# Branch A of a two-branch encoder layer: softmax sums divided out behind the value products, and GpSimd taking over weight subtractions

## The chip, the cores and the metric

One core of one Trainium2 chip runs the whole layer. The metric is the device time of one launch in microseconds (us). A change of less than about 4 us (0.2%) is what a measurement of this kernel can hardly tell from none.

## What is computed

Two inputs, `x_prompt` (1024 tokens of width 1024) and `x_sample` (512 tokens), go through the same encoder layer in float32. Branch A, which the change concerns, is grouped-query attention with 8 query heads of width 64 and 2 key/value heads:

```python
xn = rmsnorm(x); z = xn @ w_in          # q_A | k_A | v_A | q_B | k_B | v_B | gate_A | gate_B
# branch A, per key/value head (2) and query head in its group (4):
s = einsum('bqkgd,bskd->bkgqs', q, k) * scale
p = softmax(s, axis=-1)
o_A = einsum('bkgqs,bskd->bqkgd', p, v)
# branch B: 8-head attention over a clamped 8 x 16 window, with a position bias
mix = (sigmoid(gate_A) * (o_A @ w_proj_a) + sigmoid(gate_B) * (o_B @ w_proj_b)) @ w_out
x = x + mix
x = x + relu(rmsnorm(x) @ w_up) ** 2 @ w_down        # followed by a last rmsnorm
```

## The kernel before

All large products run on TensorE (PE) with operands that are split in two: a high part rounded to the product's number format, and a low part, the rest. `split` makes them: ScalarE (ACT) copies the source into the high part, VectorE (DVE) subtracts that from the source. A product of two split operands is three matmuls (`mm3`, line 214), one with a split operand on one side is two.

`run` handles one input. The 512-token input goes first (its names end in `s0`, "short"), then the 1024-token input (`s1`, "long", where `NB` is 2). After both, an MLP stage of about half the run follows. For branch A, `run` goes twice through two phases, once for each key/value group g:

- phR (projection): per 128 tokens, `zs` = q and k and v of this group (24 matmuls), `zvs` = branch B's values (24 matmuls), the norm and rotation of q and k (`chain`: `us` on GpSimd (POOL), `ts` on DVE, `rrs` on ACT), and their transposition `pqs` on PE. `load_a(g)` loads and splits this group's q, k and v weights (`wghs` high, `wgls` low).
- phA (attention). A unit is one head and 512 queries (4 units of 4 tiles of 128 queries per group in s0, 8 in s1). `s_tile` makes scores `ss` of 128 queries in PSUM (lines 801, 802), DVE takes the row maximum (`nms`, 804), ACT the exponential into `ps` with the row sum `ls` (811), DVE the reciprocal `rls` (813), and GpSimd multiplies the 128 x T tile by it (814). For units with `qb` 0 (all of s0, half of s1), `t_chunk` transposes `ps` on PE (`pTs`, 838) 128 keys at a time; ACT copies the high part `pths` (841), DVE subtracts the low part `ptls` (842). For the other half of s1, `turn_a` transposes `ps` in 32 x 32 blocks on DVE (856), writes it to DRAM (`tas`) and `fetch_a` reads it back rearranged (`hqs`); `cut_a` splits it on ACT (887) and GpSimd (889). `pv` multiplies these by the values (`os`, 825 and 826), and `finish_o` adds the upper and lower half of `os` (copy on ACT 484, addition on DVE 494 into `ot_As`) and `put` writes the result to DRAM (`oads`), as a DMA that stands in ACT's queue (439).

Between these steps PE works on filler, the matmuls of gate A (`gpss`), which `gate` hands out in pieces of three; its weights (`w_gs`) are loaded and split chunk by chunk, the next one held back until the present one is under way. 

The code's order is not the order on the engines. A scheduling layer places each instruction on its engine by its own estimate of when inputs are there, then adds semaphores; instructions pinned by `keep_in_program_order` or `issue_after` hold their place. Each engine then runs its row strictly in order, SyncE (SP) and ACT their DMA issues too. A small change in phA thus moves instructions of all engines there and in the phase behind it. Tiles come from pools with a set number of buffers (`bufs`); an instruction that writes a buffer waits until its last reader is done.

Of the kernel before, what the change touches and what calls it, by code (L numbers as in the profile page):

```python
# [11 lines left out]
F32 = mybir.dt.float32  # L12
# [3 lines left out]
ALU = mybir.AluOpType  # L16
AX = mybir.AxisListType

P = 128
D = 1024  # L20
NC8 = D // P
HD = 64
# [39 lines left out]
def encoder(ctx: ExitStack, tc: tile.TileContext, xs, outs, w):  # L62
    nc = tc.nc
    dram = ctx.enter_context(tc.tile_pool(name="dram", bufs=1, space=bass.MemoryType.DRAM))
    cst = ctx.enter_context(tc.tile_pool(name="cst", bufs=1))
    sml = ctx.enter_context(tc.tile_pool(name="sml", bufs=8))
# [26 lines left out]
    def mm(name):  # L93
        return pmm.tile([P, 512], F32, tag="mm", name=name)
# [98 lines left out]
    def behind(engine):  # L193
# [3 lines left out]
            yield  # L197
        firm[engine].clear()

    def split(hi, lo, src, pin=False):  # L200
        op = nc.scalar.activation(hi, src, AF.Copy)
        note("ACT", op)
        if pin:
            tc.keep_in_program_order(op)
        n = src.shape[1]
        cut = [0, n // 2, n] if n % 2 == 0 else [0, n]
        for a, b in zip(cut, cut[1:]):
            op = nc.vector.tensor_tensor(lo[:, a:b], src[:, a:b], hi[:, a:b].bitcast(F32), op=ALU.subtract)  # L208
            if pin:
                tc.keep_in_program_order(op)  # L210
            note("DVE", op)
# [211 lines left out]
    def run(tr, nxt, first):  # L423
        N, x, T, NT, NB = tr.N, tr.x, tr.T, tr.NT, tr.NB
        xh, xl = tr.xh, tr.xl
        rows = T // GRID_W
# [4 lines left out]
        oad = dram.tile([4 * P, T], F32, name=f"oad{N}")  # L431
# [5 lines left out]
        def put(dst, src):  # L437
            if slot_no[0] is None:
                nc.scalar.dma_start(dst, src)
            else:  # L440
                later_put.append((slot_no[0], dst, src))
# [27 lines left out]
                    put(dst[c * P : (c + 1) * P, tb * 512 : tb * 512 + 512], sg)  # L469
                    yield  # L470

        def finish_o(o, n, dst, pool, nm, parts=None):

            both = len(o.shape) == 3
            cols = 2 * n if both else n
            t = pool.tile([P, cols], F32, tag="ot", name=f"ot_{nm}", bufs=2 if cols == 512 and both else 3)
            c, b = t[0:HD, 0:n], t[0:HD, cols - n : cols]
            if both:
                tv = t[0:HD].rearrange("p (i q) -> p i q", i=2)
                nc.scalar.activation(tv, o[HD:P], AF.Copy)  # L480
                nc.vector.tensor_tensor(tv, o[0:HD], tv, op=ALU.add)
                o = b
            else:
                nc.scalar.activation(c, o[HD:P, :n], AF.Copy)
                o = o[0:HD, :n]
            if parts is not None:
                hi, lo, ps = parts
                b = t[ps, cols - n : cols]
                nc.vector.tensor_tensor(b, o, c, op=ALU.add)
                nc.scalar.activation(hi, b, AF.Copy)  # L490
                op = nc.vector.tensor_tensor(lo, b, hi.bitcast(F32), op=ALU.subtract)
                last_sum[:] = [op.ins]
                return
            nc.vector.tensor_tensor(b, o, c, op=ALU.add)
            put(dst, b)


# [41 lines left out]
        for g in range(2):  # L539
            with phase(f"phR{N}_{g}") as ph:  # L540
# [29 lines left out]
                if first and fresh:  # L570
                    warm_up(4)
                    last_sub = []

                    def first_tile(parts):
                        def hi_of(kb):
                            hi, lo, src = parts[kb]
                            tc.keep_in_program_order(nc.scalar.activation(hi, src, AF.Copy))

                        def lo_of(kb, a):
                            hi, lo, src = (t[:, 2 * a : 2 * a + 2] for t in parts[kb])  # L580
                            tc.keep_in_program_order(
                                nc.vector.tensor_tensor(lo, src, hi.bitcast(F32), op=ALU.subtract)
                            )

                        hi_of(0)
                        tr.p0_t(0, xn_of[0], [partial(lo_of, 0, 0), partial(lo_of, 0, 1)])
                        hi_of(1)
                        lo_of(1, 0)
                        last_sub.append(partial(lo_of, 1, 1))
                        warm_up(4)  # L590

                    def more_x():
                        x23 = slot([P, 2, D], F32, f"x23{N}", True)
                        for i in range(2):
                            tc.keep_in_program_order(
                                nc.sync.dma_start(x23[:, i, :], x[(2 + i) * P : (3 + i) * P, :])
                            )
                            xt_of[2 + i] = x23[:, i, :]


                    def more_and_norm():
                        more_x()
                        xn_of[1] = tr.p0(1, ph, gb, x1.pop(), last_sub.pop())

                    wh, wl = load_a(g, lambda: x1.append(norm_load(x, 1, ph, f"{N}_1")), first_tile, more_and_norm)
                    tr.p0_t(1, xn_of.pop(1))
                    xn_of[2] = tr.p0(2, ph, gb, xt_of[2])
                else:
                    with tc.issue_after(ends) if g else ExitStack():
                        wh, wl = early.pop("a") if early else load_a(g)  # L610
                if g == 0 and first:
                    setup_tables()
                if early:
# [102 lines left out]
                for tt in range(NT):  # L716
                    tb, j = divmod(tt, 4)
                    nm = f"{N}_{g}_{tt}"
# [17 lines left out]
                    op = nc.sync.dma_start(rt, w["rope"][tt * P : (tt + 1) * P])  # L736
# [51 lines left out]
                setup_bias()  # L788
            with phase(f"phA{N}_{g}") as ph:
                units = [(h, qb) for h in range(4) for qb in range(NB)]  # L790
                PP = {}

                def s_tile(u, j):
                    h, qb = u
                    nm = f"{N}_{g}_{h}_{qb}_{j}"
                    q0 = (qb * 4 + j) * P
                    lhs = qT[h % 2][:, h // 2, q0 : q0 + P]
                    s = big(f"s{nm}")[:, :T]
                    for kb in range(NB):
                        ks = slice(kb * 512, kb * 512 + 512)  # L800
                        nc.tensor.matmul(s[:, ks], lhs, kT[:, 0, ks], start=True, stop=False)
                        nc.tensor.matmul(s[:, ks], lhs, kT[:, 1, ks], start=False, stop=True)  # L802
                    nm_ = sml.tile([P, 1], F32, tag="nm", name=f"nm{nm}")
                    nc.vector.tensor_reduce(nm_, s, axis=AX.X, op=ALU.max, negate=True)  # L804
                    p = ph.tile([P, T], F32, tag="P", name=f"p{nm}", bufs=8)
                    l = sml.tile([P, 1], F32, tag="l", name=f"l{nm}")
                    to, of = p, s
                    if NB == 2 and qb == 1:
                        to = p.rearrange("p (b k i) -> p k b i", b=4, i=32)
                        of = s.rearrange("p (k i b) -> p k b i", b=4, i=32)  # L810
                    op = nc.scalar.activation(to, of, AF.Exp, bias=nm_, accum_out=l)  # L811
                    rl = sml.tile([P, 1], F32, tag="rl", name=f"rl{nm}")
                    nc.vector.reciprocal(rl, l)  # L813
                    nc.gpsimd.tensor_scalar(p, p, rl, 1.0, op0=ALU.mult, op1=ALU.mult)  # L814
                    PP[u, j] = p
                    return op.ins

                o_of = {}

                def pv(u, kc, hi, lo):  # L820
                    h, qb = u
                    if kc == 0:
                        o_of[u] = mm(f"o{N}_{g}_{h}_{qb}")
                    o = o_of[u]
                    nc.tensor.matmul(o, vhl[:, kc, :], hi, start=(kc == 0), stop=False)
                    nc.tensor.matmul(o, vhl[:, kc, :], lo, start=False, stop=(kc == NT - 1))
                    if kc == NT - 1:
                        r0 = (g * 4 + h) * HD
                        finish_o(o, 512, oad[r0 : r0 + HD, qb * 512 : qb * 512 + 512], ph, f"A{N}_{g}_{h}_{qb}")

                queue = []
                LAG = 2
# [56 lines left out]
                        nc.gpsimd.tensor_tensor(lo[:, a], lo[:, a].bitcast(F32), hi[:, a].bitcast(F32), op=ALU.subtract)  # L889

                if NB == 2:
                    for u in ((0, 1), (0, 0)):
                        for j in range(4):
                            last_exp[:] = [step_s(u, j)]
                            fill.pull(1)
                    for i in range(3):
                        fetch_a((0, 1), i)
                    for h in range(4):
                        u, nn, nd = (h, 1), (h + 1, 0), (h + 1, 1)
# [14 lines left out]
                        for kc in range(NT):  # L914
# [6 lines left out]
                            hi, lo = (t[:, :, kc % 2 * 32 : kc % 2 * 32 + 32] for t in quarter[u, kc // 2])  # L921
# [5 lines left out]
                else:  # L927
# [4 lines left out]
                    for ui, u in enumerate(units):  # L932
                        h, qb = u
# [17 lines left out]
                fill.drain()  # L951
                for item in queue:
                    pv(*item)

        mA = {}
        wp_b = []
# [1140 lines left out]
```

## Time and profile before

| | |
|---|---|
| median of 3 runs | 2106.4 us (2104.5 to 2107.51) |
| the profiled execution | 2105.4 us, its span 2103.6 us |
| granted TensorE clock | 0.999 |
| busy share of the span | PE 99%, DVE 70%, ACT 54%, POOL 21% |
| phA of s0, g 0 and 1 | about 50 to 98 us and 124 to 166 us of the span |
| phA of s1, g 0 and 1 | about 447 to 560 us and 635 to 760 us |
| phR between them | about 98 to 124 us and 560 to 635 us |

PE is nearly always occupied, so time can come only from the moments in which it waits. The profile lists who waited for whom: "PEld" is PE's weight load, which stands in the same row as the matmuls and goes ahead of its matmul. Matmuls overlap and their ends are modelled, so a wait that the weight load shows can be hidden, in the column of PE itself, under the recorded length of the matmul before. 1.8 us of the 2105.4 lie outside the span.

### The profile page before, as it was taken

To read this page: it belongs to the slowest core of one execution; us is meant where nothing else is said; L and a number is where in the kernel's file an instruction comes from. 1 tells how busy PE (TensorE), PEld (TensorE's weight loads), DVE (VectorE), ACT (ScalarE), POOL (GpSimd) and SP (SyncE) were. 2 spreads that over 40 slices of the span, in tenths; PEclk is the share of its full clock that TensorE was granted. 3 is DMA by queue.
4 is the path that set the end of the run, shared out by engine and by line. 5 is a ranking of instruction groups with operands and counts; after the bars stand their busy time and mean duration, and the time that the engine had idled before them with its cause. 6 is when DMAs were issued, how large, how long until landed. Compare 5 with 4: busy or idle time off the path is not lost. (4 is left out here: it accounts for less than half of the span.)

```text
span 2103.6 us, 31314 instructions
## 1 busy us (share of the span) xinstructions
PE 2072.8 (99%) x10615; PEld 1809.0 (86%) x10615; DVE 1477.5 (70%) x2761; ACT 1142.2 (54%) x2455; POOL 445.6 (21%) x510
## 2 busy tenths in 40 slices
PE   9999999999999999999999999999999999999998
PEld 8887878987797778888888999999999988888886
DVE  6665786778648747778854877787777777669563
ACT  6664753667566745566423556565556634334442
POOL 2232310338435823543102100011000000000000
PEclk9999999999999999999999999999999999999999
DMA  6437557557626866877553666478445899788561
GB/s 193 136 101 209 158 165 253 182 135 191 171 65 182 208 170 198 235 225 219 181 182 131 196 195 206 153 240 223 145 155 161 283 342 348 214 273 277 159 209 61
DMA packets 406758, 406.45 MB, mean 193 GB/s; under 512 B 97599, under 2 KB 333767, under 8 KB 406599
## 3 DMA queue, kind: packets, MB, share of 16 engines
q1 hardware_dynamic: 368119, 339.16, 52.8%
q10 hardware_dynamic: 31328, 45.11, 6.4%
q0 software_dynamic: 7152, 20.19, 3.5%
q8 instruction: 84, 1.38, 0.3%
q14 instruction: 75, 0.61, 0.1%
HBM read 291.06 MB, written 114.10 MB: 193 GB/s over the span
## 5 line engine op out<-in xcount | busy, mean ns | idle before, releaser
L214 PE MATMUL dn<-wd,ah 128*128 128x512 f32 x1248 | 384.4, 389 | 0.0
L214 PEld LDWEIGHTS dn<-wd,ah 128*128 128x128 f32 x1248 | 234.2, 188 | 48.7
L214 PE MATMUL dn<-wd,al 128*128 128x512 f32 x624 | 242.8, 389 | 0.0
L1571 ACT ACTIVATE ah<-ar 128x512 fp32r<-128x512 f32 x168 | 104.1, 627 | 203.3 <-PE dn L214 184.3
L214 PE MATMUL gpss<-xs_0h,w_gs 128*128 128x512 f32 x512 | 186.1, 400 | 0.3 <-DVE w_gs L208 0.2
L1572 DVE TENSOR_TENSOR al<-ar,ah 128x512 fp32r<-128x512 f32 x168 | 113.9, 686 | 71.6 <-ACT ah L1571 64.7
L214 PE MATMUL ud<-B,A 128*128 128x384 f32 x768 | 143.6, 334 | 0.7 <-DVE c L1689 0.7
L214 PE MATMUL uc<-B,A 128*128 128x384 f32 x768 | 143.7, 334 | 0.0
L214 PE MATMUL ua<-B,A 128*128 128x384 f32 x768 | 138.8, 334 | 0.0
L214 PEld LDWEIGHTS dn<-wd,al 128*128 128x128 f32 x624 | 117.1, 188 | 24.2
L214 PEld LDWEIGHTS ud<-B,A 128*128 128x128 f32 x768 | 134.0, 188 | 1.1 <-DVE c L1689 1.1
L214 PEld LDWEIGHTS uc<-B,A 128*128 128x128 f32 x768 | 134.1, 188 | 0.2 <-ACT A L1571 0.2
L214 PEld LDWEIGHTS ua<-B,A 128*128 128x128 f32 x768 | 133.7, 188 | 0.2
L180 POOL TENSOR_TENSOR rs_f<-ms_f,mhalf 128x1 f32<-128x1 f32 x6 | 4.0, 667 | 590.7 <-DVE ms_f L176 590.7
L811 ACT ACTIVATE ps<-ss,nms 128x1024 f32<-128x1024 f32 (+1 forms) x96 | 93.4, 973 | 56.4 <-DVE nms L804 46.1
L814 POOL TENSOR_SCALAR ps<-ps,rls 128x1024 f32<-128x1024 f32 (+1 forms) x96 | 97.8, 1019 | 123.6 <-DVE rls L813 105.8
L214 PE MATMUL ops<-wh_os,mgs 128*128 128x512 f32 x384 | 119.5, 391 | 0.0
L804 DVE TENSOR_REDUCE nms<-ss 128x1 f32<-128x1024 f32 (+1 forms) x96 | 99.4, 1038 | 21.7 <-PE ss L802 20.6
L214 PEld LDWEIGHTS gpss<-xs_0h,w_gs 128*128 128x128 f32 x512 | 96.2, 189 | 18.7 <-DVE w_gs L208 0.7
L214 PE MATMUL gpss<-xs_0l,w_gs 128*128 128x512 f32 x256 | 101.2, 395 | 0.0
L1571 ACT ACTIVATE A<-S 128x512 fp32r<-128x512 f32 x128 | 75.9, 624 | 31.7 <-DVE S L1634 22.9
L214 PE MATMUL gpss<-xs_1h,w_gs 128*128 128x512 f32 x256 | 90.8, 393 | 0.0
(299 smaller groups left out, 5160.9 us busy)
## 6 DMA issues: line engine op xcount, KB each, us to landing
ar<-ud SPq DMA_DIRECT2D x120, 512.0 KB, 5.3
br<-in_w_mlp_down_dram SPq DMA_DIRECT2D x72, 512.0 KB, 5.3
rawu<-in_w_mlp_up_dram SPq DMA_DIRECT2D x64, 512.0 KB, 4.1
ud<-c ACTq DMA_DIRECT2D x128, 192.0 KB, 2.6
raw_gs<-in_w_in_dram SPq DMA_DIRECT2D x32, 512.0 KB, 3.9
tas<-ps SPq DMA_DIRECT2D x32, 512.0 KB, 3.1
hqs<-tas SPq DMA_DIRECT2D x32, 512.0 KB, 6.1
ud<-cs SPq DMA_DIRECT2D x64, 192.0 KB
```

The lines of the kernel that those rows point to most:

```text
L180: op = nc.gpsimd.tensor_tensor(r[:, :n], m[:, :n], mhalf[:, :n], op=ALU.pow)
L214: op = nc.tensor.matmul(out, a, b, **kw)
L804: nc.vector.tensor_reduce(nm_, s, axis=AX.X, op=ALU.max, negate=True)
L811: op = nc.scalar.activation(to, of, AF.Exp, bias=nm_, accum_out=l)
L814: nc.gpsimd.tensor_scalar(p, p, rl, 1.0, op0=ALU.mult, op1=ALU.mult)
L1571: nc.scalar.activation(hi, src, AF.Copy)
L1572: nc.vector.tensor_tensor(lo, src, hi.bitcast(F32), op=ALU.subtract)
```

## The change

The multiplication of each 128 x T tile of exponentials by its reciprocal sum (line 814) is gone. Instead the four sums of a unit are collected in one 128 x 4 tile, inverted at once, written to DRAM as a row of 512 numbers (`rds`), read back in the same row for all 64 partitions (`rbs`, one buffer in s1, two in s0), and GpSimd multiplies the finished 64 x 512 output by it. Both DMAs stand in SP's queue. Besides, in s1's phA the low parts of the gate weights, and those of `load_a(1)`, are subtracted on GpSimd instead of DVE.

```diff
+    subtract = [nc.vector]
...
-            op = nc.vector.tensor_tensor(lo[:, a:b], src[:, a:b], hi[:, a:b].bitcast(F32), op=ALU.subtract)
+            op = subtract[0].tensor_tensor(lo[:, a:b], src[:, a:b], hi[:, a:b].bitcast(F32), op=ALU.subtract)
...
-        def finish_o(o, n, dst, pool, nm, parts=None):
+        def finish_o(o, n, dst, pool, nm, parts=None, scale=None):
...
             nc.vector.tensor_tensor(b, o, c, op=ALU.add)
+            if scale is not None:
+                nc.gpsimd.tensor_tensor(b, b, scale, op=ALU.mult)
             put(dst, b)
...
+                        subtract[0] = nc.gpsimd if NB == 2 and g else nc.vector
                         wh, wl = early.pop("a") if early else load_a(g)
+                        subtract[0] = nc.vector
...
-                    l = sml.tile([P, 1], F32, tag="l", name=f"l{nm}")
+                    if j == 0:
+                        L4[u] = ph.tile([P, 4], F32, tag="l4", name=f"l{nm}", bufs=4)
+                    l = L4[u][:, j : j + 1]
...
                     op = nc.scalar.activation(to, of, AF.Exp, bias=nm_, accum_out=l)
-                    rl = sml.tile([P, 1], F32, tag="rl", name=f"rl{nm}")
-                    nc.vector.reciprocal(rl, l)
-                    nc.gpsimd.tensor_scalar(p, p, rl, 1.0, op0=ALU.mult, op1=ALU.mult)
                     PP[u, j] = p
+                    if j == 3:
+                        rl = ph.tile([P, 4], F32, tag="r4", name=f"rl{nm}", bufs=3)
+                        nc.vector.reciprocal(rl, L4.pop(u))
+                        rd[u] = dram.tile([4, P], F32, name=f"rd{nm}")
+                        nc.sync.dma_start(rd[u].rearrange("j p -> p j"), rl)
...
                     if kc == 0:
                         o_of[u] = mm(f"o{N}_{g}_{h}_{qb}")
+                        rows = ph.tile([P, 512], F32, tag="rb", name=f"rb{N}_{g}_{h}_{qb}", bufs=3 - NB)
+                        nc.sync.dma_start(rows[0:HD], rd.pop(u).rearrange("j p -> (j p)").partition_broadcast(HD))
+                        rb_of[u] = rows[0:HD]
...
                 if NB == 2:
+                    subtract[0] = nc.gpsimd
...
                 for item in queue:
                     pv(*item)
+                subtract[0] = nc.vector
```

What this does to the rows of the engines is shown at three places. The first is GpSimd's row in phA of s1, group 0, around the end of head 0. Names are `tile`, input, group, head, query half, tile or quarter; the last number of a name is a buffer. Before:

```order
L889 TENSOR_TENSOR hqs1_0_0_1_5680<-hqs1_0_0_1_5680 128x512 x2
L814 TENSOR_SCALAR ps1_0_1_1_2_5795<-ps1_0_1_1_2_5795,rls1_0_1_1_2_5798 128x1024
L889 TENSOR_TENSOR hqs1_0_0_2_5682<-hqs1_0_0_2_5682 128x512 x2
L814 TENSOR_SCALAR ps1_0_1_1_3_5841<-ps1_0_1_1_3_5841,rls1_0_1_1_3_5844 128x1024
L889 TENSOR_TENSOR hqs1_0_0_3_1_5753<-hqs1_0_0_3_1_5753,hqs1_0_0_3_0_5752 128x512 x2
L814 TENSOR_SCALAR ps1_0_1_0_0_5878<-ps1_0_1_0_0_5878,rls1_0_1_0_0_5881 128x1024
L814 TENSOR_SCALAR ps1_0_1_0_1_5898<-ps1_0_1_0_1_5898,rls1_0_1_0_1_5901 128x1024
```

And GpSimd's row at the same place in the changed kernel:

```order
L902 TENSOR_TENSOR hqs1_0_0_0_5592<-hqs1_0_0_0_5592 128x512 x2
L210 TENSOR_TENSOR w_gs1_2304_2_5667<-raw_gs1_2304_2_0_5665,w_gs1_2304_2_5667 128x512 x2
L902 TENSOR_TENSOR hqs1_0_0_1_5594<-hqs1_0_0_1_5594 128x512 x2
L902 TENSOR_TENSOR hqs1_0_0_2_5596<-hqs1_0_0_2_5596 128x512 x2
L902 TENSOR_TENSOR hqs1_0_0_3_1_5660<-hqs1_0_0_3_1_5660,hqs1_0_0_3_0_5659 128x512 x2
L498 TENSOR_TENSOR ot_As1_0_0_0_5804<-ot_As1_0_0_0_5804,rbs1_0_0_0_5673 64x512
L902 TENSOR_TENSOR hqs1_0_1_0_5846<-hqs1_0_1_0_5846 128x512 x2
```

The 128 x 1024 multiplications between the cuts of `hqs` are gone; a pair of gate subtractions and one 64 x 512 multiplication per unit came in.

The second is ACT's row there, around the write of the unit's output. Before:

```order
L484 ACTIVATE ot_As1_0_0_0_5906<-os1_0_0_0_5765 64x512
L811 ACTIVATE ps1_0_1_0_0_5878,ls1_0_1_0_0_5879<-ss1_0_1_0_0_5871,nms1_0_1_0_0_5876 128x1024
L468 ACTIVATE sgs1_2304_1_0_5967<-gpss1_2304_1_0_5761 128x512
L439 DMA zgs1_0_4591<-sgs1_2304_1_0_5967 128x512
L811 ACTIVATE ps1_0_1_0_1_5898,ls1_0_1_0_1_5899<-ss1_0_1_0_1_5891,nms1_0_1_0_1_5896 128x1024
L439 DMA oads1_4593<-ot_As1_0_0_0_5906 64x512
L811 ACTIVATE ps1_0_1_0_2_5917,ls1_0_1_0_2_5918<-ss1_0_1_0_2_5910,nms1_0_1_0_2_5915 128x1024
```

ACT's row at the same place in the changed kernel:

```order
L486 ACTIVATE ot_As1_0_0_0_5804<-os1_0_0_0_5672 64x512
L819 ACTIVATE ps1_0_1_0_1_5800,ls1_0_1_0_0_5784<-ss1_0_1_0_1_5793,nms1_0_1_0_1_5798 128x1024
L441 DMA oads1_4529<-ot_As1_0_0_0_5804 64x512
L819 ACTIVATE ps1_0_1_0_2_5816,ls1_0_1_0_0_5784<-ss1_0_1_0_2_5809,nms1_0_1_0_2_5814 128x1024
L819 ACTIVATE ps1_0_1_0_3_5838,ls1_0_1_0_0_5784<-ss1_0_1_0_3_5831,nms1_0_1_0_3_5836 128x1024
```

The write `oads`, which now also waits for GpSimd's multiplication, stands one exponential behind the copy of `os` instead of two exponentials, a tanh and another write behind it; the exponentials of the next unit stand behind it.

The third is PE's row in s0, from the last `zvs` of group 1's phR to its first scores. Before, the transpositions of token block 1 and 2 stand ahead of the last `zvs` (24 matmuls each):

```order
L633 MATMUL pqs0_1_2_1585<-ident_88,rrs0_1_2_1450 128x128 x3
L214 MATMUL zvs0_1_3_1595<-wh_vs0_1_0_1051,xs0_0h0_158 128x256
L214 MATMUL zvs0_1_3_1595<-wl_vs0_1_0_1052,xs0_0h0_158 128x256
L214 MATMUL zvs0_1_3_1595<-wh_vs0_1_0_1051,xs0_0l0_160 128x256
L214 MATMUL zvs0_1_3_1595<-wh_vs0_1_0_1051,xs0_0h0_158 128x256
```

In PE's row of the changed kernel they stand singly among the matmuls of the last `zvs`, that of block 0 first:

```order
L216 MATMUL zvs0_1_3_1563<-wl_vs0_1_0_1024,xs0_0h0_158 128x256
L639 MATMUL pqs0_1_0_1388<-ident_88,rrs0_1_0_1272 128x128
L216 MATMUL zvs0_1_3_1563<-wh_vs0_1_0_1023,xs0_0l0_160 128x256
L216 MATMUL zvs0_1_3_1563<-wh_vs0_1_0_1023,xs0_0h0_158 128x256
L216 MATMUL zvs0_1_3_1563<-wl_vs0_1_0_1024,xs0_0h0_158 128x256
L639 MATMUL pqs0_1_0_1388<-ident_88,rrs0_1_0_1272 128x128
```

All transpositions of this phase moved behind the `zvs` of blocks 1 and 2, and 33 matmuls of gate A stand between that of block 2 and the first scores, where 18 stood before.

More of the change, by code (lines that the diff above doesn't have):

```diff
@@ L790, in run @@
                 units = [(h, qb) for h in range(4) for qb in range(NB)]
-                PP = {}
+                PP, L4, rd = {}, {}, {}
                 def s_tile(u, j):
@@ L811, in s_tile @@
                     op = nc.scalar.activation(to, of, AF.Exp, bias=nm_, accum_out=l)
-                    rl = sml.tile([P, 1], F32, tag="rl", name=f"rl{nm}")
-                    nc.vector.reciprocal(rl, l)
-                    nc.gpsimd.tensor_scalar(p, p, rl, 1.0, op0=ALU.mult, op1=ALU.mult)
                     PP[u, j] = p
+                    if j == 3:
[3 more added lines that the diff above has]
+                        nc.sync.dma_start(rd[u].rearrange("j p -> p j"), rl)
                     return op.ins
-                o_of = {}
+                o_of, rb_of = {}, {}
                 def pv(u, kc, hi, lo):
@@ L828, in pv @@
                         r0 = (g * 4 + h) * HD
-                        finish_o(o, 512, oad[r0 : r0 + HD, qb * 512 : qb * 512 + 512], ph, f"A{N}_{g}_{h}_{qb}")
+                        finish_o(o, 512, oad[r0 : r0 + HD, qb * 512 : qb * 512 + 512], ph, f"A{N}_{g}_{h}_{qb}", None, rb_of.pop(u))
                 queue = []
```

## The prediction

> **What bounds the kernel now.** I read the page's head first, then the view of busy time by stretches, then who waited for whom on PE.
>
> ```profile
> span 2103.6 us, 31314 instructions
> core 0: us, PE busy (x) PEld busy (x) DVE busy (x) ACT busy (x) POOL busy (x), PEclk, DMA share, GB/s
> 98.00:124.00 26.00, 26.00 (x182) 25.70 (x182) 13.24 (x36) 16.30 (x81) 9.17 (x12) 1.00 0.30 100
> 447.00:560.00 113.00, 107.08 (x511) 82.11 (x510) 92.75 (x130) 82.45 (x131) 78.20 (x64) 1.00 0.74 191
> 635.00:760.00 125.00, 120.62 (x570) 92.79 (x569) 90.36 (x129) 83.79 (x133) 78.30 (x65) 1.00 0.75 196
> ```
>
> The two last rows are phA of s1, with PE idle for 5.9 and 4.4 us; the 26 us of phR have no idle at all. So the change can win only what PE loses in phA. The idle column undercounts that, as PE's timeline shows on a stretch without waits:
>
> ```profile
> 757.00 0.62 PE L214 MATMUL pqbs<-xs_0h,w_bqs 128*128 128x512 f32 x2
> 757.45 0.39 PE L214 MATMUL pqbs<-xs_0l,w_bqs 128*128 128x512 f32 x1
> 757.68 0.62 PE L214 MATMUL pqbs<-xs_0h,w_bqs 128*128 128x512 f32 x2
> ```
>
> A matmul is recorded as 0.39 us long, yet three start in 0.68 us, one each 0.227 us. Up to 0.16 us of every wait lies under the record of the matmul ahead. The weight loads do not overlap so; their waits are the better measure of loss. Over the whole run (us in all, times, longest), from the view of waits of PEld and then of PE:
>
> ```profile
> PEld pTs L838 <- DVE ptls L842: 8.5, 10, 1.8
> PEld ss L801 <- ACT ps L811: 8.1, 20, 1.3
> PEld pTs L838 <- POOL ps L814: 7.8, 16, 0.8
> PEld os L826 <- DVE ptls L842: 3.8, 7, 0.8
> PEld pTs L838 <- DVE ot_As L494: 2.6, 8, 0.8
> PEld os L825 <- ACT pths L841: 2.0, 6, 0.6
> PE pTs L838 <- POOL ps L814: 2.3, 7, 0.4
> ```
>
> All of these lie in phA. The first six add to 32.8 us; that is the ceiling. Three causes: DVE's low parts come late (8.5 + 3.8 = 12.3), the scores' PSUM waits for the exponential (8.1), the transposition waits for GpSimd's multiplication (7.8).
>
> **The change part by part.** The sum is made against the profiled execution, 2105.4 us (span 2103.6 and 1.8 around it); the median of the runs, 2106.4, is 1.0 above it, and I add that at the end.
>
> *The multiplication of `ps` leaves.* It is 96 instructions of 1.02 us on GpSimd, second row below, and it stood between exponential and transposition.
>
> ```profile
> L811 ACT ACTIVATE ps<-ss,nms 128x1024 f32<-128x1024 f32 (+1 forms) x96 | 93.4, 973 | 56.4 <-DVE nms L804 46.1
> L814 POOL TENSOR_SCALAR ps<-ps,rls 128x1024 f32<-128x1024 f32 (+1 forms) x96 | 97.8, 1019 | 123.6 <-DVE rls L813 105.8 <-PE pTs L838 8.7 <-PE ss L802 7.3
> L889 POOL TENSOR_TENSOR hqs<-hqs 128x512 fp32r<-128x512 f32 x48 | 61.8, 1309 | 11.9 <-ACT hqs L887 9.8 <-PE pTs L838 2.0
> ```
>
> GpSimd's own time costs nothing, it is idle most of the run. The gain is the wait of `pTs`: at least the 2.3 us of PE's column, at most the 7.8 of the weight loads. By the overlap above the true value is near the upper end; but next in line is the exponential itself, which is 1.0 us earlier and not free, and the transpositions now stand closer behind it. I take 6.0.
>
> *DVE gets lighter.* The view of groups of DVE in 447 to 560 us has what goes:
>
> ```profile
> L813 DVE RECIPROCAL rls<-ls 128x1 f32<-128x1 f32 x32 | 4.7, 147 | 4.1 <-ACT ps L811 4.0
> L208 DVE TENSOR_TENSOR wgls<-rawqs,wghs 128x512 fp32r<-128x512 f32 x4 | 5.0, 1280 | 1.5 <-ACT wghs L201 1.5
> L208 DVE TENSOR_TENSOR wgls<-rawkvs,wghs 128x256 fp32r<-128x256 f32 x4 | 3.6, 934 | 0.1
> L208 DVE TENSOR_TENSOR w_gs<-raw_gs,w_gs 128x512 fp32r<-128x512 f32 x4 | 3.3, 856 | 0.3 <-ACT w_gs L201 0.3
> L856 DVE STREAM_TRANSPOSE ps<-ps 128x1024 f32<-128x1024 f32 x16 | 19.8, 1238 | 5.3 <-POOL ps L814 5.2
> L804 DVE TENSOR_REDUCE nms<-ss 128x1 f32<-128x1024 f32 x32 | 38.9, 1214 | 8.3 <-PE ss L802 8.3
> ...
> L208 DVE TENSOR_TENSOR w_gs<-raw_gs,w_gs 128x512 fp32r<-128x512 f32 x6 | 4.7, 796 | 0.3 <-ACT w_gs L201 0.3
> ```
>
> Of 32 reciprocals 8 stay: 24 x 0.147 = 3.5 us. The subtractions go whole: 5.0 + 3.6 + 3.3 = 11.9. Besides, DVE stands still 4.0 us for the exponential ahead of a reciprocal and 5.2 ahead of a transpose until GpSimd has multiplied; both go or shrink. DVE is busy for 92.75 of 113 us there; its free time grows from 20 to about 36 us, of which 9 less are spent in front of a waiting instruction. In group 1 (the last row, from 635 to 760 us) it is 3.5 and four of its gate subtractions of 0.8 (3.2), with the same two waits. So the late low parts (12.3 us) become rarer, not gone: the row maximum (1.2 us) and the block transposes (1.24) still stand in DVE's row between an ACT copy and its subtraction. Bounds 0 and 12.3; half of it, 6.0, since about half of DVE's idle and held time is new.
>
> Some of those subtractions are long for a reason:
>
> ```profile
> 551.81 1.78 DVE L208 TENSOR_TENSOR wgls<-rawqs,wghs 128x512 fp32r<-128x512 f32 x1
> 554.86 2.84 DVE L208 TENSOR_TENSOR wgls<-rawkvs,wghs 128x256 fp32r<-128x256 f32 x2
> 551.38 3.36 POOL L889 TENSOR_TENSOR hqs<-hqs 128x512 fp32r<-128x512 f32 x2 [1.25 <-ACT hqs L887]
> L208 DVE TENSOR_TENSOR wgls<-rawqs,wghs x12: 679/688/1780, 69.8 to 551.8; 128x512 fp32r<-128x512 f32 x12
> ```
>
> Beside GpSimd's cuts of `hqs` the subtraction takes 1.78 us where its median is 0.69, and the pair of cuts 3.36 where two means are 2.62. On one engine they stand one behind the other. The Trainium skill's page "SBUF — State Buffer", section "Who interferes with whom", says that a DVE instruction with two SBUF inputs and a GpSimd instruction that reads SBUF exclude one another for the whole instruction; the rows agree. By that rule no such pair is left in s1's phA, and the sum would be that of the first rival below; by DVE's row with subtractions of 0.69 alone, it would be mine with 3 us less of DVE relief.
>
> *Scores waiting for exponentials (8.1).* In the same stretch ACT waits:
>
> ```profile
> ACT ps L811 <- DVE nms L804: 17.7, 14, 3.3
> ACT ps L811 <- DVE rls L813: 5.0, 6, 1.3
> ACT hqs L887 <- DMA hqs<-tas: 0.4, 1, 0.4
> ```
>
> The second goes with the reciprocals. The first follows from PE's order and DVE's 1.2 us maximum and mostly stays. Bounds 0 and 8.1; by the share 5.0 of 22.7 I take 2.0.
>
> *GpSimd's new work.* 24 multiplications of 64 x 512, and in s1 12 subtractions of 128 x 512 and 4 of 128 x 256; the nearest row is the cut, 1.31 us. In 447 to 560 us: 78.2 - 32 x 1.12 (36) + 8 x 1.31 + 8 x 1.31 + 4 x 0.65 = about 66 of 113 us. Not a bound. But ACT's DMA `oads` now waits for it, with exponentials and `pths` copies queued behind:
>
> ```profile
> 549.14 0.59 ACT L484 ACTIVATE ot_As<-os 64x512 f32<-64x512 f32 x1
> 550.61 0.67 DVE L494 TENSOR_TENSOR ot_As<-os,ot_As 64x512 f32<-64x512 f32 x1
> 551.32 0.46 ACTq L439 DMA_DIRECT2D oads<-ot_As  x1
> 543.52 0.17 DVE L813 RECIPROCAL rls<-ls 128x1 f32<-128x1 f32 x1 [1.33 <-ACT ps L811]
> 562.21 0.68 DVE L494 TENSOR_TENSOR ot_As<-os,ot_As 64x512 f32<-64x512 f32 x1 [1.84 <-ACT ot_As L484]
> ```
>
> The write followed DVE's addition by 0.04 us; now it comes 1.3 us later, and 3.9 if GpSimd has just begun a pair of cuts. ACT is idle for 30.6 of the 113 us, 3.8 per unit, which covers the usual case, since the next exponential waits for a maximum anyway. Bounds 0 and, if half of the extra 3.9 us reached PE in each of the 24 units, 47. I take 0.125 us a unit, near the lower end because of that idle time: 3.0 lost.
>
> *The row through DRAM.* 48 more DMAs in SP's row. The write has runs of 4 bytes, 512 of them; the nearest rows:
>
> ```profile
> biases<-shifted SPq DMA_DIRECT2D x8, 384.0 KB, 5.5
> rts<-in_rope_dram SPq DMA_DIRECT2D x24, 64.0 KB, 2.5
> ```
>
> A DMA with 2048 short runs lands after 5.5 us, one of 128 runs after 2.5: write and read together take 5 to 11. The last reciprocal of the unit (3,0) ran at 543.5, its sum was ready at 562.9, 19 us later. The page "DMA: Bandwidth & Descriptors" of the Trainium skill, section "Specifications", speaks against such runs: below 512 bytes a write becomes read-modify-write; no row here separates that, and the sum would be the same by it, as long as the pair stays under 19 us. In SP's row, `hqs` and weight loads queue behind a `rds` that waits for its reciprocal and a `rbs` that waits for the buffer of the unit before. The `hqs` are fetched a unit ahead. Cost 0, at most the one wait of `hqs` for its DMA, 0.4 us in ACT's rows above, per group.
>
> *phR of s0, group 1.* The head transpositions stand behind two more `zvs`; gate A's matmuls fill in, so PE's work is the same, but 15 of its fillers are used up early. Six scalings `rrs` of 0.33 us (2.0) have to fit beside eight matmuls ahead of the first `pqs`.
>
> ```profile
> L712 ACT ACTIVATE rrs<-ts,rs_As x144: 331/334/383, 31.3 to 624.8; 128x64 f32<-128x64 f32 x144
> ```
>
> Bounds 0 and 4 (two such gaps); I take 1.5 lost.
>
> Sum: 2105.4 - 6.0 - 6.0 - 2.0 + 3.0 + 1.5 = 2095.9; with the 1.0 of the median, **2096.9 us**.
>
> **Rivals.** (1) *DVE and GpSimd no longer collide, and all late low parts go*: the full 12.3 and 7.8 with 2.0, less the 4.5: 2105.4 - 22.1 + 4.5 + 1.0 = 2088.8. For it: the 1.78 and 2.84 us rows stand among the waits. Against: most of `ptls`'s lateness lies outside such collisions, and the maxima stay. This is the rule of "SBUF — State Buffer" worked out. Chance 0.15.
>
> (2) *The waits keep their place under new names*: the scheduler moves the transpositions up to the exponential, and only the 2.3 us of PE's column are won while 1.5 is lost in phR: 2105.4 - 2.3 + 1.5 + 1.0 = 2105.6. For it: PE waits 8.1 us for exponentials already. Against: DVE's relief is real work. Chance 0.22.
>
> (3) *Slower: ACT stands at `oads` until GpSimd has multiplied.* With two pairs of cuts or subtractions ahead (5.2 us) and its own 1.3, less the 1.1 us exponential between, ACT is held for 5.4 us, 1.6 over the 3.8 that it has free per unit. It decides from there on: in all 16 units of s1 that is 26, less the 14.0 gained, plus 1.5: 2105.4 + 13.5 + 1.0 = 2119.9; in 12 of them, 2113.5. For it: the write has moved closer to the copy. Against: the changed row of GpSimd has at most two pairs ahead of a multiplication and most were asked for earlier. Chance 0.10.
>
> **How the numbers follow.** My forecast has the remaining 0.53. The range 2088 to 2107 holds it, rival 2 and about half of rival 1; below lie the other half (0.07), above rival 3 (0.10). Alone, the forecast reaches from 2092 (DVE relief 9, ACT loss 1) to 2102 (relief 3, ACT loss 5). A measurement tells 0.2%, 4.2 us, from no change. Faster by more: 0.52 of the forecast, all of rival 1, 0.01 of rival 2: 0.68. Within: 0.01 and 0.20, 0.21. Slower: rival 3 and 0.01 of rival 2, 0.11.
>
> **What would show it.** Right: no PE wait for GpSimd at `pTs`; the waits for `ptls` at half; DVE under 80 us busy in s1's first phA; both long phA stretches shorter by 4 to 7 us each in the place where group 1's phR begins. Wrong: ACT with long waits for `ot_As` on GpSimd at the write (rival 3), or `pTs` waiting for ACT's exponentials as long as for GpSimd before (rival 2). phR of s0 longer by more than 2 us, or `hqs` waits of ACT on DMA above 2 us, would break the two costs that I put near nothing.

## The result, and the profile after

The changed kernel takes 2230.3 us (median of 6 runs, 2224.2 to 2230.8) against 2106.3 before: 1.0583 times as long (95% interval 1.0569 to 1.0597), 124 us more. The prediction had 2096.9 and a range up to 2107; it was wrong in sign.

The head of the page after, and the view of the cores:

```profile
span 2228.1 us, 31175 instructions
core 0: 2228.1 us, clock 0.974
```

The clock was 0.999 before. Then busy time by stretches (columns as in the prediction), cut at the phases of the kernel after: phA of s0 group 0, phR, phA of group 1 up to its last value product; then the same three of s1.

```profile
51.00:106.00 55.00, 46.14 (x208) 36.64 (x208) 31.54 (x56) 31.32 (x63) 2.57 (x2) 0.88 0.47 81
106.00:149.00 43.00, 39.88 (x239) 36.74 (x238) 16.12 (x40) 18.36 (x88) 11.64 (x14) 0.96 0.46 139
149.00:209.00 60.00, 43.94 (x190) 33.64 (x190) 30.31 (x52) 29.05 (x61) 3.80 (x3) 0.88 0.41 88
489.00:649.00 160.00, 130.29 (x562) 101.56 (x561) 82.48 (x96) 83.37 (x133) 61.72 (x51) 0.88 0.86 148
649.00:710.00 61.00, 61.00 (x418) 60.57 (x417) 30.09 (x78) 36.05 (x170) 19.62 (x25) 1.00 0.30 78
712.00:880.00 168.00, 127.85 (x561) 100.39 (x560) 88.90 (x102) 83.52 (x133) 55.37 (x43) 0.88 0.80 144
```

In every stretch of phA PE stands idle for 9 to 40 us, the clock is at 0.88, and DVE, ACT and GpSimd are not busier than before. The DMA engines are: in s1 a share of 0.86 and 0.80, where 0.74 and 0.75 stood before, while they move 148 and 144 GB/s instead of 191 and 196. They work more and move less. phR of s1 (649 to 710) is as it was. Measured on PE's own landmarks (from the last `pqs` of a phR to the last value product or the next `zs`), the four stretches of phA grew from 43.9, 43.1, 126.4 and 124.7 us to 56.8, 63.7, 161.9 and 169.7, and phR of s0's group 1 from 32.2 to 42.3. Together that is 124 us, the whole loss.

The view of waits says for what:

```profile
ACT hqs L900 <- DMA hqs<-tas: 83.1, 19, 8.3
POOL ot_As L498 <- DMA rbs<-rds: 58.1, 3, 37.9
ACT wghs L203 <- DMA rawqs<-in_w_in_dram: 11.7, 2, 6.7
PEld pTs L851 <- DVE ptls L855: 39.1, 12, 7.8
PEld os L838 <- ACT pths L854: 23.8, 9, 6.6
```

In the kernel before, ACT waited 0.9 us in all for `hqs`; now it waits 83.1. What PE waits for are ACT's and DVE's copies, which are late because those engines stand behind a load. The queue of SP in the first phA shows where it begins; the last row is GpSimd's:

```profile
59.75 0.39 SPq L825 DMA_DIRECT2D rds<-rls  x1
60.22 1.39 SPq L509 DMA_DIRECT2D rawqs<-in_w_in_dram  x1
65.44 0.37 SPq L825 DMA_DIRECT2D rds<-rls  x1
72.02 0.48 SPq L835 DMA_DIRECT2D rbs<-rds  x1
72.59 0.54 SPq L509 DMA_DIRECT2D rawqs<-in_w_in_dram  x1
81.56 0.46 SPq L835 DMA_DIRECT2D rbs<-rds  x1
81.86 1.28 POOL L498 TENSOR_TENSOR ot_As<-ot_As,rbs 64x512 f32<-64x512 f32 x1 [37.86 <-DMA rbs<-rds]
```

The write of the first row of 2 KB is issued at 59.75; its read is issued 12.3 us later, and the product can use it at 81.86, 22 us after the write. The two loads of `rawqs` stand 12.4 us apart, the second behind a read that waits. That leaves three theories. In A the write itself holds up the DMA engines. In B SP's row stands at `rbs` until `rds` has landed. In C, the prediction's own rival 3, GpSimd's multiplication and ACT's write behind it are to blame.

For A there is one more reading: the trace's record of single DMA packets. KB that all queues moved in each us after the last packet of a row's write (left: its time), in the kernel after, for two of the 24 writes:

```
 61.2    0   31    4    5   36   53   40   23   26   43  111  337  206
501.4  135  246    4    4    8   20   16   12   12   25  318   10  115
```

In these two the 512 packets are sent within 1 us, at 8 ns each in the record, and then all other traffic crawls for 8 to 10 us. PE has work for some 10 us and then stands, and the clock goes down. By stretches, around the write at 501:

```profile
501.50:511.50 10.00, 10.00 (x52) 8.04 (x51) 6.83 (x8) 6.30 (x11) 0.00 (x0) 1.00 0.95 52
511.50:515.30 3.80, 1.25 (x8) 0.81 (x6) 0.13 (x1) 0.00 (x0) 0.00 (x0) 1.00 0.62 167
515.30:525.50 10.20, 5.38 (x16) 3.98 (x16) 3.55 (x4) 3.20 (x5) 4.96 (x4) 0.50 1.28 137
```

DMA engines 0.95 busy at 52 GB/s; then PE busy for 1.25 of 3.8 us; then the clock at 0.50 for 10.2 us. (The share adds up the recorded times of packets, and these can overlap: it reads 1.28 in the last row. So it is a measure of load, not a part of a fixed whole.)

### The profile page after: what moved, and what is told of

Read it like the earlier page. It is cut to its first block, busy times and chain, and to the rows that moved or that the text cites. A ratio compares the mean times of both kernels' runs of the same rounds, so it can differ in the third digit from the quotient of the medians.

```text
span 2228.1 us, 31175 instructions
## 1 busy us (share of the span) xinstructions
PE 2110.4 (95%) x10615; PEld 1840.0 (83%) x10615; DVE 1460.7 (66%) x2673; ACT 1143.9 (51%) x2455; POOL 396.3 (18%) x454
## 4 chain that ended last, share of the span: by engine, by line
PE 68%; DMA 8%; DVE 1%; issue 1%; ACT 1%; SPq 1%; POOL 0%; ACTq 0%; POOLq 0%; DVEq 0%
PE dn L216 19%; PE ua L216 6%; PE ud L216 6%; PE uc L216 6%; PE gpss L216 6%; DMA hqs<-tas 4%; PE ops L216 4%; PE ub L216 3%; DMA tas<-ps 3%; PE zs L216 2%; PE ppbs L216 2%; PE ppas L216 2%; PE pqbs L216 2%; PE pkbs L216 2%; PE zvs L216 2%; PE dnf L216 1%
## 5 line engine op out<-in xcount | busy, mean ns | idle before, releaser
L216 PE MATMUL gpss<-xs_0h,w_gs 128*128 128x512 f32 x512 | 191.7, 413 | 1.1 <-ACT sgs L470 0.6
L851 PE MATMUL pTs<-ident,ps 128*128 128x128 f32 x384 | 71.2, 310 | 43.3 <-DVE ptls L855 38.7
L855 DVE TENSOR_TENSOR ptls<-pTs,pths 128x512 fp32r<-128x512 f32 x96 | 63.5, 679 | 73.5 <-ACT pths L854 73.4
L851 PEld LDWEIGHTS pTs<-ident,ps 128*128 128x128 f32 x384 | 55.9, 162 | 63.9 <-DVE ptls L855 39.1
```

The lines of the kernel that those rows point to most:

```text
L216: op = nc.tensor.matmul(out, a, b, **kw)
L851: nc.tensor.transpose(pt[:, j * P : (j + 1) * P], PP[u, j][:, kc * P : (kc + 1) * P], ident)
L855: nc.vector.tensor_tensor(lo, pt, hi.bitcast(F32), op=ALU.subtract)
```

## The experiments

All times are medians; ratios are to the kernel before on the same chip.

| run | us | ratio | interval |
|---|---|---|---|
| e1_no_row | 2101.6 | 0.9980 | 0.9970 to 0.9989 |
| e2_runs_of_16 | 2105.3 | 0.9996 | 0.9987 to 1.0005 |
| e3_write_unread | 2216.0 | 1.0513 | 1.0488 to 1.0538 |
| e4_before_and_write | 2212.1 | 1.0514 | 1.0486 to 1.0542 |
| f1_write_spread | 2103.1 | 0.9984 | 0.9974 to 0.9994 |
| f2_write_128 | 2177.8 | 1.0339 | 1.0318 to 1.0361 |
| f3_write_64_apart | 2102.0 | 0.9977 | 0.9967 to 0.9988 |
| g1_no_row_dve | 2109.1 | 1.0011 | 1.0002 to 1.0020 |
| g2_subs_alone | 2106.5 | 1.0001 | 0.9992 to 1.0010 |
| g5_row_long_only | 2096.0 | 0.9951 | 0.9938 to 0.9963 |
| h3_row_long_pool_write | 2095.1 | 0.9946 | 0.9933 to 0.9960 |
| h1_no_row_pool_write | 2092.4 | 0.9936 | 0.9922 to 0.9949 |

### Which part of the change costs

**e1_no_row**

```diff
-    rd[u] = dram.tile([4, P], F32, name=f"rd{nm}")
-    nc.sync.dma_start(rd[u].rearrange("j p -> p j"), rl)
...
-    rows = ph.tile([P, 512], F32, tag="rb", ...)
-    nc.sync.dma_start(rows[0:HD], rd.pop(u).rearrange("j p -> (j p)").partition_broadcast(HD))
-    rb_of[u] = rows[0:HD]
+    rb_of[u] = ones[0:HD]
```

> The changed kernel without the row through DRAM: neither `rds` nor `rbs` is issued, and GpSimd multiplies the finished output by a tile of ones (so the division is left out; every other instruction of the change stays). Theory A (the write of 512 runs of 4 bytes holds up the DMA engines for some 10 us per unit) and theory B (SP's row stands at `rbs` until `rds` has landed, and issues late what stands behind) both expect what the prediction had without this row: about 2097 us, 2090 to 2106. Theory C (the multiplication on GpSimd and the write of ACT that waits for it, with the subtractions, are what costs) expects most of the 124 us to stay: above 2180.

2101.6 us, inside the range that A and B gave. The row through DRAM is the loss; everything else of the change together is 0.2% faster than before. Theory C is out as the cause of the 124 us.

**e3_write_unread**

```diff
-    nc.sync.dma_start(rows[0:HD], rd.pop(u).rearrange("j p -> (j p)").partition_broadcast(HD))
+    nc.sync.dma_start(rows[0:HD], bass.AP(tensor=win.tensor, offset=win.offset, ap=[[0, HD], [1, 512]]))
```

> The changed kernel with `rds` as it is, but `rbs` reads 512 numbers of an input instead of it (the division is left out), so nothing waits for the write to land. Theory A: the writes still hold up every load behind them, most of the loss stays: 2180 to 2230 us. Theory B: the wait in SP's row is gone and the loss with it: 2095 to 2115. Theory C: the multiplication no longer waits for the row, so it is about 2100 to 2130.

2216.0 us. With nothing waiting for the write, 110 of the 124 us stay. By this run theory B has the other 14 at most.

**e4_before_and_write**, made from the kernel before:

```diff
     PP[u, j] = p
+    if j == 3:
+        row = dram.tile([4, P], F32, name=f"rd{nm}")
+        nc.sync.dma_start(row.rearrange("j p -> p j"), rl.to_broadcast([P, 4]))
```

> The kernel before, with one thing added: after the fourth tile of each unit SP writes 512 runs of 4 bytes to DRAM (a copy of the last reciprocal, four times for each partition), and nobody reads or waits for it. Theory A: 24 writes hold up the loads and `tas` and `hqs` by some 10 us each; at least half of the 124 us, 2165 to 2230. Theory B and theory C: no wait is added, 2102 to 2112.

2212.1 us, 106 more than before, for 24 writes of 2 KB that nobody reads. Nothing else of the change is in this kernel. That settles A against B and C for the larger part. Between 60 and 70 us, just behind the first write, its stretch reads as follows; the row behind it is that of the kernel before.

```profile
60.00:70.00 10.00, 10.00 (x56) 8.27 (x55) 7.26 (x16) 6.48 (x16) 3.47 (x5) 1.00 0.32 25
```

```profile
60.00:70.00 10.00, 10.00 (x56) 8.27 (x55) 7.35 (x17) 8.20 (x20) 3.47 (x5) 1.00 0.36 116
```

25 GB/s against 116, in a stretch where PE does the same work; the loads that are late there are felt later.

### What it is about this write

**e2_runs_of_16**, from the changed kernel:

```diff
-    rd[u] = dram.tile([4, P], F32, name=f"rd{nm}")
-    nc.sync.dma_start(rd[u].rearrange("j p -> p j"), rl)
+    rd[u] = dram.tile([P, 4], F32, name=f"rd{nm}")
+    nc.sync.dma_start(rd[u], rl)
...
-    nc.gpsimd.tensor_tensor(b, b, scale, op=ALU.mult)
+    bv = b.rearrange("d (j p) -> d j p", j=4)
+    nc.gpsimd.tensor_tensor(bv, bv, scale, op=ALU.mult)      # scale: rows read back, "d (p j) -> d j p"
```

> The changed kernel with the row laid out in DRAM as 128 runs of 16 bytes instead of 512 of 4; read back as one row as before, and GpSimd takes it with a stride. Theory A: the cost goes by the number of short runs, a quarter stays, 2097 + 133/4 = about 2130 us (2115 to 2150). Theory B: the row still makes two trips, one after the other, and `rbs` still stands in SP's row for them: above 2180. Theory C: no change, 2225 to 2235.

2105.3 us, below all three ranges: not a quarter of the loss stayed, as theory A had it, but almost none. So the cost doesn't simply go by the number of runs.

**f1_write_spread** (below, [4, P, 128] and each run 512 bytes from the next), **f3_write_64_apart** ([4, P, 16], 64 bytes) and **f2_write_128** ([1, P], 128 runs side by side), all from the kernel before:

```diff
     if j == 3:
-        row = dram.tile([4, P], F32, name=f"rd{nm}")
-        nc.sync.dma_start(row.rearrange("j p -> p j"), rl.to_broadcast([P, 4]))
+        row = dram.tile([4, P, P], F32, name=f"rd{nm}")
+        nc.sync.dma_start(row[:, :, 0:1].rearrange("j p o -> p j o"), rl.to_broadcast([P, 4])...)
```

> The kernel before and the same 24 unread writes of 512 runs of 4 bytes, but each run lands 512 bytes from the next instead of side by side. Theory A1 (neighbouring runs share a line of memory and are written one after the other): the loss is gone, 2102 to 2115 us. Theory A2 (each short run costs the engine some 0.3 us wherever it lands): as with the runs side by side, 2195 to 2230.

> The kernel before and 24 unread writes of 128 runs of 4 bytes side by side, a quarter of the runs. Theory A2: each write holds up the loads for 10/4 = 2.5 us instead of 10, which the loads' lead mostly covers: 2106 to 2125 us. Theory A1: 128 runs in a quarter of the lines, as many to a line as before, also a quarter: the same. A theory A3, in which any write below some run length costs its 10 us however many runs it has, expects 2190 to 2220.

> The kernel before and 24 unread writes of 512 runs of 4 bytes, each run 64 bytes from the next (512 bytes apart cost nothing, side by side 106 us). If runs only disturb each other within 64 bytes, it costs nothing: 2100 to 2110 us. If within 512 bytes, 8 runs share what 128 shared before; between the two, 2110 to 2150, as 128 runs of 16 bytes side by side, 32 to 512 bytes, cost some 4.

2103.1, 2177.8 and 2102.0 us. In e4, f1, f2 and f3 the instructions stand in the same order on all five engines, and in e4 and f3 the packets are the same to within one (419430 and 419431). Only the addresses differ there, and with runs 64 bytes from start to start the 106 us are gone. A quarter of the runs, side by side, still costs 71 (f2, two executions, 2173.0 and 2182.5), two thirds of e4's 106; that lies between the ranges of A1 and A2 and the one of A3, so none of the three had it right. The same ten microseconds in f2, then f3:

```profile
60.00:70.00 10.00, 9.97 (x54) 8.30 (x55) 7.35 (x16) 6.78 (x16) 3.48 (x5) 1.00 0.44 77
```

```profile
60.00:70.00 10.00, 10.00 (x56) 8.26 (x55) 7.35 (x17) 8.20 (x20) 3.46 (x5) 1.00 0.58 157
```

77 and 157 GB/s, after 25 in e4. So runs of 4 bytes are slow where they lie side by side; 64 or 512 bytes apart they are not, and neither are runs of 16 bytes side by side. That neighbours in one small piece of memory are written one after the other, that several pieces are written at a time, and that the engines' queues stand meanwhile, fits all five layouts; it is my reading, since no trace shows the memory itself. How large such a piece is stays open. With 64 bytes, 16 runs share it in e4 and f2, 4 in e2 (which then cost almost nothing) and one in f3; with 16 bytes, 4 in e4 and f2 and one in e2 and f3. Runs of 4 bytes were not tried at spacings between 4 and 64 bytes.

The Trainium skill's page "DMA: Bandwidth & Descriptors", section "Specifications", says that below 512 bytes the DMA engine reads, modifies and writes. By that rule alone e4 and f3 would cost the same; they differ by 110 us, and the measurement decides.

### The rest of the prediction's sum

**g1_no_row_dve** and **g2_subs_alone**: e1 with, on DVE, the subtractions that the change moved; and the kernel before with these subtractions on GpSimd.

```diff
 # g1, from e1
-    subtract[0] = nc.gpsimd if NB == 2 and g else nc.vector
+    subtract[0] = nc.vector
...
-    subtract[0] = nc.gpsimd
 # g2, from the kernel before: the split and the assignments of `subtract` as in the change
+    subtract[0] = nc.gpsimd
```

> The changed kernel without the row through DRAM (a tile of ones in its place, the division is left out) and with the low parts of the weights subtracted on DVE as before: the moved sums alone. By the terms of the prediction the subtractions were most of DVE's relief; without the row and with them the kernel took 2101.6 us. Theory P (the prediction's): without them it is slower, 2103 to 2106. Theory Q (the subtractions on GpSimd give nothing, or cost by standing ahead of the cuts of `hqs`): 2097 to 2102.

> The kernel before with the subtractions on GpSimd alone; the tile's multiplication, reciprocals and sums stay. Theory P: DVE is lighter by 12 us in the first long stretch and the late low parts go by a third: 2101 to 2104 us. Theory Q: GpSimd is busy with the multiplications (78 of 113 us in that stretch), its cuts and multiplications come later: 2106 to 2115.

2109.1 and 2106.5 us. Against e1 the subtractions on GpSimd are worth some 7 us; in g2, where GpSimd still multiplies the tiles, nothing. Theory P was right in g1 in direction (2103 to 2106 was said, more came) and wrong in g2, which lies in theory Q's range; neither part gains by itself.

**g5_row_long_only**, the row of e2 in s1 only:

```diff
     PP[u, j] = p
-    if j == 3:
+    if NB == 1:
+        rl = sml.tile([P, 1], F32, tag="rl", name=f"rl{nm}")
+        nc.vector.reciprocal(rl, l)
+        nc.gpsimd.tensor_scalar(p, p, rl, 1.0, op0=ALU.mult, op1=ALU.mult)
+    elif j == 3:
```

> The changed kernel with the row as 128 runs of 16 bytes, and only in s1; s0 keeps the multiplication of each tile as before. With the row in both inputs the long stretches of phA were 5.7 and 5.4 us shorter than before and the phR ahead of them 1.3, and phR of s0's second group 11.4 longer. Theory R (the s1 gain is the change's own and stays; the loss lies in s0's order and goes): 2106 - 12.4 = about 2094 us, 2091 to 2098. Theory S (the order falls anew and the gain is not the change's own): 2101 to 2107.

2096.0 us, theory R. In e2 the phR of s0's second group took 43.6 us, here 32.2 as before. The two long stretches of g5, by the windows that the prediction used, and its waits of PEld:

```profile
447.00:560.00 113.00, 110.54 (x538) 87.84 (x537) 81.45 (x95) 82.09 (x132) 60.79 (x48) 1.00 0.75 199
635.00:760.00 125.00, 123.12 (x594) 98.48 (x594) 86.35 (x108) 83.38 (x132) 63.13 (x49) 1.00 0.78 207
```

```profile
PEld ss L808 <- ACT ps L820: 5.2, 16, 0.8
PEld os L845 <- ACT pths L861: 5.0, 7, 1.8
PEld pTs L858 <- DVE ptls L862: 4.9, 10, 1.3
PEld pTs L858 <- POOL ps L825: 2.4, 5, 0.8
```

PE's idle time there is 2.5 and 1.9 us, from 5.9 and 4.4. The phases themselves take 120.4 and 119.4 us, from 126.4 and 124.7.

**h1_no_row_pool_write** (from e1) and **h3_row_long_pool_write** (from g5):

```diff
-    put(dst, b)
+    if scale is not None:
+        nc.gpsimd.dma_start(dst, b)
+    else:
+        put(dst, b)
```

> As the run without the row (a tile of ones, the division left out; 2101.6 us, where ACT stood up to 3.7 us at the write behind GpSimd's cuts and multiplication, and PE lost 8.9 us to late copies, with the clock halved three times), and GpSimd issues the write `oads` itself. Theory T: these three stops and their half clock go, some 10 us: 2090 to 2094. Theory U: 2099 to 2104.

> As the run with the row in s1 only, and in s1 GpSimd itself issues the write `oads` behind its multiplication instead of ACT, so ACT does not stand there. Theory T (ACT's standing at that write, up to 2.6 us at a time with exponentials and copies behind it, reaches PE): 4 to 8 us less than that run, 2087 to 2091. Theory U (it is covered, or GpSimd's own issue takes its place in front of the cuts of `hqs`): within 2 us of it or slower.

2092.4 and 2095.1 us. In e1 this is what GpSimd and ACT did, first two rows GpSimd's:

```profile
490.50 5.05 POOL L900 TENSOR_TENSOR hqs<-hqs 128x512 fp32r<-128x512 f32 x4 [9.21 <-ACT hqs L898]
495.49 1.27 POOL L498 TENSOR_TENSOR ot_As<-ot_As,oness 64x512 f32<-64x512 f32 x1
```

```profile
496.80 0.45 ACTq L441 DMA_DIRECT2D oads<-ot_As  x1
497.35 1.08 ACT L852 ACTIVATE pths<-pTs 128x512 fp32r<-128x512 f32 x2 [3.69 <-POOL ot_As L498]
```

Two pairs of cuts, the multiplication, and only then ACT's write, with PE's copies behind it: rival 3, word for word, but at three places and not in all units. The three stops (3.1 to 3.7 us of ACT, 1.9 to 2.5 us in PE's column) each had 3.4 us of half clock behind them. With the write on GpSimd's own queue e1 loses 9.2 us (theory T), with no half clock left. In g5, where the order kept the stops ahead of copies and exponentials at 2.6 us and under (one of 4.3 us stands ahead of a copy of weights), it is within 0.9 us (theory U). h3 has the lowest time here of the kernels that leave nothing out; it and g5 beat the kernel before and the kernel after, and these runs do not tell one from the other.

## Why the prediction was wrong, point by point

- **The step that failed: "The row through DRAM ... Cost 0".** Measured against e1, which lacks only this row, it cost 2230.3 - 2101.6 = 128.7 us. The bound was sought at the nearest row by duration, 5.5 us for `biases`, taken for 2048 short runs; but the packet record of the kernel before has it as 128 packets of 3072 bytes, so that row says nothing of 512 runs of 4 bytes. And the question asked was whether the pair lands within 19 us and what stands behind it in SP's row. The first pair took 22. But the larger part is that the write slows all traffic: alone, in e4, it cost 106 us. Both signs that the prediction named against this step and against its term for phR of s0 came: ACT waited 83.1 us for `hqs`, and phR of s0 grew by 10.1.
- **Why so much of it.** An estimate, argued and not shown by a run: over the whole of s1's two phA, by PE's landmarks, the DMA share before was 0.69 of 126.3 us and 0.72 of 124.8, that is 87 and 90 us of load. 8 writes at 9.5 us, if all are like the two in the packet record, are 76. Together that is 163 and 166 us; the phases took 161.9 and 169.7. So phA seems to have become bound by the DMA engines. The shares of 0.74 and 0.75 had stood in the rows that the prediction quoted, and no term used them.
- **A term that the sum lacked: the clock.** 0.974 of 2228.1 us means 58 us of full clock missing, an upper limit for what half clock added, since PE stood idle in part of it. Every half-clock piece in these runs, but the one that each run ends with, is 3.4 us long or a multiple of it (up to 13.7). The gap of PE ahead of it can be shorter: 2.4, 1.9 and 2.5 us in PE's column in e1, 2.6 in e2. Nor does every gap bring one: one of 3.4 us in e4, at 528.8, did not. Page "TensorE: Matmul & The Clock Gate" of the Trainium skill, section "Part 1: The HAM clock gate", has the clock at half after an idle window of about 3.4 us. The length of the pieces agrees with such a window; the gaps of 1.9 to 2.6 us do not agree with it as the least idle time, and the measurement decides.
- **The range.** The bounds of this term were 0 and 0.4 us per group, since only SP's row was asked. No rival held a write that hurts other traffic, and a cost with no like in the trace deserved a chance of its own.
- **The s1 terms, read in g5.** The next four items compare waits in g5 with those before. g5's instructions have an order of their own, so this supports the terms but does not prove them for the changed kernel; e1, which has the change without the row, won 4.6 us, as three stops of ACT took back what h1 prices at 9.2.
- **The multiplication leaves (6.0).** In g5 PEld's wait for it fell from 7.8 to 2.4 us, all of that in s0, which kept it: 5.4. That fits.
- **DVE gets lighter (6.0).** Waits for `ptls` 12.3 (two rows) to 4.9: 7.4; DVE 81.45 busy where under 80 was forecast. The size fits, but it needs both parts: g2 won nothing and g1 lost 3.
- **Scores behind exponentials (2.0).** 8.1 to 5.2: 2.9. That fits.
- **ACT at the write (3.0).** In g5 the copies' wait grew from 2.0 to 5.0, by 3.0; in e1, h1 prices it at 9.2. The mechanism was right; its size hangs on where the order puts two pairs of cuts ahead of a multiplication.
- **phR of s0 (1.5, bounds 0 and 4).** 10.1 in the kernel after and 11.4 in e2; 0 in e1 and g5. Too small. The view of e2 by stretches has it:

```profile
122.00:127.00 5.00, 2.23 (x9) 1.39 (x8) 3.78 (x9) 4.20 (x14) 3.59 (x5) 0.73 0.00 0
127.00:132.00 5.00, 5.00 (x15) 3.93 (x14) 4.78 (x12) 2.07 (x6) 0.00 (x0) 0.59 0.85 281
```

PE stands 2.8 us, because the rotation of block 2 is late, and then the clock halves; the bound had the gap but not the clock behind it. GpSimd's wait for the row is not what holds block 2 there, as its row in e2 shows:

```profile
96.13 1.56 POOL L499 TENSOR_TENSOR ot_As<-ot_As,rbs 64x512 f32<-64x512 f32 x1 [4.39 <-DVE ot_As L496]
121.03 1.17 POOL L703 TENSOR_TENSOR us<-ts,rts 128x160 f32<-128x160 f32 x2 [15.22 <-issue]
```

The last product with a row in that phase begins at 96.13; when GpSimd begins block 2's part, it has stood idle for 15.2 us. So block 2 waited for other engines there, whose order had changed. No run kept the whole row in s0 together with the old order, so what each does alone is not shown.
- **Rivals.** (1) and (2) were about the remainder: their prices of 2088.8 and 2105.6 lie on both sides of what g5 gave, 2096.0. That g5 comes so near to the forecast of 2096.9 is in part luck: g5 leaves s0 as it was, with neither the 1.5 us lost in phR nor the gain there that the sum had, and the whole change with runs of 16 bytes (e2) took 2105.3. (3) exists in e1, at three places instead of twelve, and is not what made the changed kernel slow.

## What to carry to other kernels

Ask of every small write to DRAM how many of its runs lie side by side, and lay a column written from many partitions out so that each partition's numbers lie together (here 16 bytes, 124 us to nothing), or put the runs 64 bytes apart. Weigh such a write against the DMA share of its stretch, not against the row of the queue that issues it: here 8 to 10 us behind a write came, 8 times in each phA of s1, on top of a share of 0.7 (by the estimate above). And a gap of PE of 2 to 3 us can cost more than itself, as the clock behind it may be halved for 3.4 us or longer.

## What the runs showed of the hardware that I had not expected

- 512 runs of 4 bytes side by side slowed all DMA traffic for 8 to 10 us where it was read (23 to 25 GB/s instead of 116 to 157 in the same ten microseconds), although their own packets are recorded at 8 ns each and the engines as partly idle (share 0.32 to 0.36 there, 0.95 elsewhere). The same packets 64 bytes apart cost nothing that shows.
- f1 and f3, with 24 added writes, ran 0.2% faster than the kernel before (intervals below 1). The added instructions move the order on every engine; 3 to 5 us of any difference between kernels of differing code may be no more than that, the 0.2% of e1 included.
